# Second expert weights loaded as two whole rows a partition, in a transformer block with a mixture of experts

## The chip, the cores and the metric

The kernel runs on one core of a Trainium2 chip, as one launch. The metric is the time of the launch on the device in microseconds; lower is better. All data are float32 in the chip's memory (HBM); a core has an on-chip store of 128 partitions (SBUF), a smaller one for the results of products (PSUM), a matrix engine (TensorE, PE in the profile), three engines for elementwise work (VectorE as DVE, ScalarE as ACT, GpSimd as POOL), a synchronizing engine whose queue issues transfers (SyncE, SP), and 16 DMA engines that move the data.

## The reference, cut to what matters

Two transformer blocks on a sequence of 256 tokens of width 1024: a feed-forward layer, three kinds of attention and a second feed-forward layer; then a second block of long convolutions and a recurrence, and last a mixture of 16 experts, which is where the change lies. Each expert picks the 32 tokens that have the largest affinity to it:

```python
def expert_choice_moe(h, p):
    cap = EC_CAPACITY * T // N_EXPERTS                      # 2 * 256 // 16 = 32
    affinity = jax.nn.softmax((h @ p['router_w']).astype(jnp.float32), axis=-1)
    gates, idx = lax.top_k(jnp.swapaxes(affinity, 1, 2), cap)
    xe = jax.vmap(lambda hb, ib: hb[ib])(h, idx)
    hid = jax.nn.silu(jnp.einsum('becd,edf->becf', xe, p['exp_w1'])) * jnp.einsum('becd,edf->becf', xe, p['exp_w3'])
    ye = jnp.einsum('becf,efd->becd', hid, p['exp_w2']) * gates[..., None].astype(h.dtype)
    return jax.vmap(lambda ib, yb: jnp.zeros((T, D), yb.dtype).at[ib.reshape(-1)].add(yb.reshape(-1, D)))(idx, ye)
```

An expert's first and third weights (`exp_w1`, `exp_w3`) have 1024 rows of 2048 numbers, its second weights (`exp_w2`) 2048 rows of 1024 numbers. Each of the three is 8 MB, so the sixteen experts read 384 MB.

## The kernel before

Everything up to the mixture of experts takes a little over the first half of the time and is left as it is. The last function, `moe`, first finishes the token mixer's output, works out the affinities, and picks the tokens: `phr` holds for each expert a selection of 32 tokens, `ph` the same times the gates. `xeT` holds the chosen tokens of all experts, transposed.

Then a loop runs over the 16 experts. All weights of the experts come through one ring of 19 slots of 128 partitions x 2048 numbers (1 MB a slot). `wload` (line 1770) takes the next slot and issues one load of 1 MB on SP's queue; the order of the slots is fixed by `RINGS` and `RING_ORDER`, and a load waits until the products that read its slot's last content are done. There are 24 loads an expert: 8 of first weights, 8 of third weights, 8 of second weights.

First and third weights (lines 1780 to 1791): load k holds rows 128k to 128k+127, one row of 8 KB in each partition. The 32 chosen tokens of the expert are the stationary operand of products that fill 32 columns of the array; the four quarters g of the row go to four column groups, so `ps` holds quarter g in its partitions 32g to 32g+31.

Between them and the second weights (lines 1799 to 1814): the gated activation `th`, [32g + token, 512], four transposes of it (line 1805) that give `hid`, [128, q, 32g + token], and the transposed, gated selection `pgT`, which repeats each expert's 32 tokens four times over the partitions.

Second weights (lines 1815 to 1827): row f = 512g + 128q + p of the weights belongs to partition p of `hid`'s part (q, g). The output's 1024 columns are taken in two halves `nh` of 512. For each half and each q one load brings, for partition p, the four rows of g = 0 to 3, and of each row the half's 512 numbers: four pieces of 2 KB. Four products, one for each g, add into four column groups of one PSUM tile `pe2`. After the four loads of a half, ScalarE copies `pe2` to `ye` (line 1825), and two products over all 128 partitions (line 1827) sum the four groups, apply the gates, and scatter the tokens into the accumulators `acc[t][nh]` (t: the two blocks of 128 tokens), which add up over all experts.

After the last expert (lines 1828 to 1848): a row `m5p` is loaded behind the weights; for each of the four accumulators, in the order (nh, t) = (0,0), (0,1), (1,0), (1,1), ScalarE sums the squares and VectorE multiplies by `m5p`; then come two inverse norms, the residual, and four stores. The helper `then` (line 1635 in the profile) keeps the order of these operations on each engine.

The order of the loads is the order of the program's lines; the tile framework's scheduler orders the instructions of the engines.

Of the kernel before, what the change touches and what calls it, by code (L numbers as in the profile page):

```python
# [11 lines left out]
F32 = mybir.dt.float32  # L12
# [3 lines left out]
AF = mybir.ActivationFunctionType  # L16
# [6 lines left out]
NE = 16  # L23
# [142 lines left out]
def _body(nc, tc, ctx, A, out):  # L166
    V, S, G, PE = nc.vector, nc.scalar, nc.gpsimd, nc.tensor
# [9 lines left out]
    psT = ctx.enter_context(tc.tile_pool(name="psT", bufs=2, space=PSUM))  # L177
# [3 lines left out]
    def consts(name, shape, src=None, eng=None):  # L181
        t = keep.tile(list(shape), F32, name=name)
        (eng or S).dma_start(t, src if src is not None else A[name])
        return t
# [11 lines left out]
    ident = consts("ident", [128, 128])  # L196
# [1402 lines left out]
    def moe(xs, w1, po, m2p, xr, rw, m3c, a2c, last):  # L1599
        with ExitStack() as fx:  # L1600
# [13 lines left out]
            for k in range(KC):  # L1614
                PE.matmul(ps[:, :NE], m3c[:, k:k + 1].to_broadcast([128, 128]), rw[:, k, :], start=(k == 0),
                          stop=(k == KC - 1))
# [103 lines left out]
            def slot():  # L1720
                used[0] += 1
                return order[(used[0] - 1) % len(order)].tile([128, 2048], F32, name="ring")
# [12 lines left out]
            pt = psT.tile([128, 4, 128], F32, name="tr")  # L1735
# [7 lines left out]
            def select(half):  # L1743
                es = slice(half * HE, half * HE + HE)
                for t in range(2):
                    V.tensor_tensor(phr[:, t, es], pos[:, t, es].unsqueeze(2).to_broadcast([128, HE, CAP]),
                                    iota.unsqueeze(1).to_broadcast([128, HE, CAP]), op=ALU.is_equal)
                    G.tensor_tensor(ph[:, t, es], phr[:, t, es].bitcast(F32),
                                    aff[:, t, es].unsqueeze(2).to_broadcast([128, HE, CAP]), op=ALU.mult)

            def gather(half, k0, n):


                es = slice(half * HE, half * HE + HE)
                ps = psM.tile([128, 2, HE * CAP], F32, name="mm")
                for k in range(k0, k0 + n):
                    j = k - k0
                    for t in range(2):
                        for h_ in (h2h, h2l):
                            PE.matmul(ps[:, j, :], h_[t][:, k * 128:(k + 1) * 128], phr[:, t, es].rearrange("p a b -> p (a b)"),  # L1760
                                      start=(t == 0 and j == 0 and h_ is h2h), stop=(t == 1 and h_ is h2l),
                                      skip_group_check=True)
                    dst = xeT[:, k, half * HE * CAP:(half + 1) * HE * CAP]
                    if k % 2:
                        S.activation(dst, ps[:, j, :], AF.Identity, scale=a2c[:, k:k + 1], bias=m3c[:, k:k + 1])
                    else:
                        V.tensor_scalar(dst, ps[:, j, :], a2c[:, k:k + 1], m3c[:, k:k + 1], op0=ALU.mult, op1=ALU.add)


            def wload(src, shape):  # L1770
                r = slot()
                v = r.rearrange("p (a b) -> p a b", b=shape)
                with tc.issue_after(last):
                    nc.sync.dma_start(v, src)
                return v

            for e in range(NE):
                es = slice(e * CAP, (e + 1) * CAP)
                pss = []
                for nm in ("exp_w1_2", "exp_w3_2"):  # L1780
                    ps = psX.tile([128, 512], F32, name="px")
                    for k in range(KC):
                        if e == 0 and nm == "exp_w1_2" and k in GATHERS:
                            if k == 0:
                                select(0)
                            gather(0, k, GATHERS[k])
                        wt = wload(A[nm][e, k * 128:(k + 1) * 128, :].rearrange("p (a n) -> p a n", a=1), 2048)
                        for g in range(4):
                            PE.matmul(ps[32 * g:32 * g + 32, :], xeT[:, k, es], wt[:, 0, g * 512:(g + 1) * 512],  # L1789
                                      start=(k == 0), stop=(k == KC - 1), skip_group_check=True)  # L1790
                    pss.append(ps)
                    if e == 0 and nm == "exp_w1_2":
                        select(1)
                        for k in range(0, KC, 2):
                            gather(1, k, 2)
                        f2.close()
                        tmp = fx.enter_context(tc.tile_pool(name="moe_t", bufs=2))
                        acc = [[psM.tile([128, 512], F32, name="mm") for _ in range(2)] for _ in range(2)]
                th = tmp.tile([128, 512], F32, name="mth")
                S.activation(th, pss[0], AF.Tanh, scale=0.5)  # L1800
                V.scalar_tensor_tensor(th, th, 1.0, pss[0], op0=ALU.add, op1=ALU.mult)  # L1801
                V.scalar_tensor_tensor(th, th, 0.5, pss[1], op0=ALU.mult, op1=ALU.mult)  # L1802
                pt = psT.tile([128, 4, 128], F32, name="tr")
                for q in range(4):
                    PE.transpose(pt[:, q, :], th[:, q * 128:(q + 1) * 128], ident)
                hid = tmp.tile([128, 4, 128], F32, name="hid")
                V.tensor_copy(hid, pt)
                pt = psX.tile([128, 512], F32, name="px")
                for t in range(2):
                    rep = tmp.tile([128, 4, CAP], F32, name="rep")  # L1810
                    V.tensor_copy(rep, ph[:, t, e:e + 1, :].to_broadcast([128, 4, CAP]))
                    PE.transpose(pt[:, t * 128:(t + 1) * 128], rep.rearrange("p a b -> p (a b)"), ident)
                pgT = tmp.tile([128, T], F32, name="pgT")
                S.activation(pgT, pt[:, :T], AF.Copy)
                wv = A["exp_w2_2"][e].rearrange("(g q p) n -> q p g n", g=4, q=4)
                for nh in range(2):
                    ns = slice(nh * 512, nh * 512 + 512)
                    pe2 = psT.tile([128, 512], F32, name="tr")
                    for q in range(4):
                        w2t = wload(wv[q, :, :, ns], 512)  # L1820
                        for g in range(4):
                            PE.matmul(pe2[32 * g:32 * g + 32, :], hid[:, q, 32 * g:32 * g + 32], w2t[:, g, :],  # L1822
                                      start=(q == 0), stop=(q == 3), skip_group_check=True)
                    ye = tmp.tile([128, 512], F32, name="ye")
                    S.activation(ye, pe2, AF.Copy)  # L1825
                    for t in range(2):
                        PE.matmul(acc[t][nh], pgT[:, t * 128:(t + 1) * 128], ye, start=(e == 0), stop=(e == NE - 1))  # L1827
            m5p = slot()[:, 0:D]
            mod_row(m5p, 5, nc.sync)
            junk = slot()  # L1830
# [73 lines left out]

    ffn(xt, hT2, None, A["ffn2_w_gate"], A["ffn2_w_up"], A["ffn2_w_down"], {-1: filter_and_modulation, HOOK2: lambda: next(mods[1]), HOOK3: lambda: next(mods[1], None)}, norm_mod)
    moe(xt, w1, *mixer2(xt, hT3, *spec, spx, w1, rowp[0]))
```

## Time and profile before

| | |
|---|---|
| median of 3 runs | 2192.0 us (2189.52 to 2193.94) |
| profiled execution, its own time | 2195.16 us |
| its span, first to last instruction | 2193.4 us |
| mean granted TensorE clock | 0.86 |
| PE busy | 1784.5 us (81%) |
| DVE, ACT, POOL busy | 884.9, 589.9, 334.8 us |
| moved | 600.95 MB, mean 274 GB/s |
| loads of expert weights | 384 of 1024 KB |

The profile is of one execution. A time in it is in microseconds from the start of the span. An engine is busy while it executes; the profile names for an idle stretch what ended it (the releaser). A product in float32 leaves two records for each matmul instruction, so the four products on one load are eight records. The DMA share of a window is the sum of the times of all its packets over 16 engines, so it can be a little above 1. In an instruction's name, out<-in are the program's tile names; 128*32 is the part of the array that a product uses (rows * columns).

### The profile page before, as it was taken

What the parts mean: (1) busy time and instruction counts of PE and PEld (TensorE: products, weight loads), DVE (VectorE), ACT (ScalarE), POOL (GpSimd) and SP (SyncE); (2) the same over time, 40 slices, a digit from 0 to 9 for tenths busy, and PEclk for the clock granted to TensorE, in tenths of its full rate; (3) what the DMA queues carried; (4) which work ended last, traced back from release to release, by engine and by line L of the source; (5) the groups of instructions that cost most, each with busy time, mean ns of one, the idle gap of its engine ahead of it and who ended that gap; (6) DMA issues with size and microseconds to landing.
All of it is one profiled execution on the core that took longest, in us unless ns stands there. A gap on an engine that the chain in (4) does not pass through costs nothing.

```text
span 2193.4 us, 28407 instructions
## 1 busy us (share of the span) xinstructions
PE 1784.5 (81%) x11441; PEld 1067.1 (49%) x11442; DVE 884.9 (40%) x1611; ACT 589.9 (27%) x954; POOL 334.8 (15%) x332
## 2 busy tenths in 40 slices
PE   7999989999988999998898877766666676666765
PEld 5889867778768877886677411111111111111111
DVE  4567865965757765787655400000000000000001
ACT  3345443445436534363233200000000000000000
POOL 2111014110325640144233100000000000000000
PEclk9999989999989999999898887677778777777677
DMA  8655546444458846433347999999999999999997
GB/s 300 224 171 149 160 138 190 138 142 127 132 170 264 292 157 200 127 105 107 92 155 264 347 406 406 410 411 410 408 407 406 407 407 407 410 411 411 409 406 278
DMA packets 237046, 600.95 MB, mean 274 GB/s; under 512 B 35384, under 2 KB 91217, under 8 KB 204146
## 3 DMA queue, kind: packets, MB, share of 16 engines
q1 hardware_dynamic: 200464, 551.89, 68.6%
q0 software_dynamic: 10496, 36.08, 5.0%
q10 hardware_dynamic: 25954, 11.16, 1.9%
q8 instruction: 90, 1.47, 0.3%
q14 instruction: 42, 0.34, 0.0%
HBM read 593.25 MB, written 9.75 MB: 275 GB/s over the span
## 4 chain that ended last, share of the span: by engine, by line
DMA 43%; PE 39%; DVE 9%; ACT 3%; issue 3%; POOL 2%; SPq 0%; ACTq 0%; DVEq 0%; POOLq 0%
DMA ring<-exp_w 38%; PE mm L302 4%; PE mm L301 3%; PE mm L299 3%; PE mm L287 3%; PE mm L288 3%; PE mm L289 3%; DVE wl L246 2%; PE mm L346 2%; PE mm L349 2%; PE mm L345 2%; PE px L1789 2%; PE tr L1822 1%; DMA wraw<-w_in 1%; ACT wh L245 1%
## 5 line engine op out<-in xcount | busy, mean ns | idle before, releaser
L1789 PE MATMUL px<-ring,xeT 128*32 128x512 f32 x2048 | 365.5, 806 | 182.6 <-DMA ring<-exp_w 182.4
L246 DVE TENSOR_TENSOR wl<-wraw,wh 128x1024 fp32r<-128x1024 f32 (+2 forms) x243 | 317.8, 1309 | 169.0 <-ACT wh L245 163.4
L245 ACT ACTIVATE wh<-wraw 128x1024 fp32r<-128x1024 f32 (+2 forms) x243 | 254.9, 1050 | 378.9 <-PE mm L301 156.2
L302 PE MATMUL mm<-hh,wl 128*128 128x256 f32 x912 | 266.7, 294 | 16.1 <-DVE wl L246 15.1
L1789 PEld LDWEIGHTS px<-ring,xeT 128*32 128x32 f32 x2048 | 49.4, 122 | 469.2 <-DMA ring<-exp_w 427.8
L299 PE MATMUL mm<-hh,wh 128*128 128x256 f32 x912 | 265.0, 291 | 2.3 <-ACT hh L245 2.3
L301 PE MATMUL mm<-hl,wh 128*128 128x256 f32 x912 | 263.0, 289 | 1.9 <-DVE hl L246 1.8
L1801 DVE SCALAR_TENSOR_TENSOR mth<-mth,px 128x512 f32<-128x512 f32 x16 | 11.0, 688 | 576.4 <-ACT mth L1800 576.4
L1822 PE MATMUL tr<-ring,hid 128*32 128x512 f32 x1024 | 175.0, 791 | 76.7 <-DMA ring<-exp_w 64.0
L302 PEld LDWEIGHTS mm<-hh,wl 128*128 128x128 f32 x912 | 177.9, 196 | 31.2 <-DVE wl L246 20.0
L299 PEld LDWEIGHTS mm<-hh,wh 128*128 128x128 f32 x912 | 178.7, 196 | 11.6 <-issue 6.9
L301 PEld LDWEIGHTS mm<-hl,wh 128*128 128x128 f32 x912 | 178.6, 196 | 7.0 <-issue 4.1
L1825 ACT ACTIVATE ye<-tr 128x512 f32<-128x512 f32 x32 | 19.1, 598 | 573.2 <-PE tr L1822 573.2
L1635 POOL TENSOR_SCALAR rsz<-ss 128x1 f32<-128x1 f32 x2 | 0.6, 301 | 955.5 <-ACT ring L1635 955.5
L288 PE MATMUL mm<-wl,hh 128*128 128x512 f32 (+2 forms) x320 | 127.9, 400 | 5.3 <-DVE wl L271 3.3
L1822 PEld LDWEIGHTS tr<-ring,hid 128*32 128x32 f32 x1024 | 26.6, 126 | 206.4 <-DMA ring<-exp_w 153.5
L289 PE MATMUL mm<-wh,hl 128*128 128x512 f32 (+2 forms) x320 | 125.4, 392 | 0.0
L287 PE MATMUL mm<-wh,hh 128*128 128x512 f32 (+2 forms) x320 | 118.9, 404 | 5.2 <-DVE wi L525 3.3
L1802 DVE SCALAR_TENSOR_TENSOR mth<-mth,px 128x512 f32<-128x512 f32 x16 | 11.0, 688 | 257.4 <-PE px L1789 257.4
L1827 PE MATMUL mm<-ye,pgT 128*128 128x512 f32 x128 | 89.6, 838 | 24.0 <-ACT ye L1825 24.0
L1800 ACT ACTIVATE mth<-px 128x512 f32<-128x512 f32 x16 | 9.6, 597 | 283.1 <-PE px L1789 283.1
L1827 PEld LDWEIGHTS mm<-ye,pgT 128*128 128x128 f32 x128 | 29.1, 252 | 88.1 <-ACT ye L1825 63.6
(757 smaller groups left out, 2735.8 us busy)
## 6 DMA issues: line engine op xcount, KB each, us to landing
ring<-exp_w SPq DMA_DIRECT2D x384, 1024.0 KB
wraw<-w_in SPq DMA_DIRECT2D x107, 512.0 KB
mraw<-mod_w POOLq DMA_DIRECT2D x48, 512.0 KB, 5.1
wraw<-ffn_w_gate SPq DMA_DIRECT2D x44, 512.0 KB
wraw<-ffn_w_up SPq DMA_DIRECT2D x44, 512.0 KB
wraw<-ffn_w_down SPq DMA_DIRECT2D x44, 512.0 KB
wraw<-w_out SPq DMA_DIRECT2D x11, 512.0 KB
skew<-bd POOLq DMA_DIRECT2D x1, 3840.0 KB, 27.3
```

Source lines behind the costliest of these rows:

```text
L245: S.activation(dst_h, src, AF.Copy)
L246: (eng or V).tensor_tensor(dst_l, src, dst_h.bitcast(F32), op=ALU.subtract)
L287: PE.matmul(ps[t], hh[:, k, sl], wh, start=(k == 0), stop=False)
L288: PE.matmul(ps[t], hh[:, k, sl], wl, start=False, stop=False)
L289: PE.matmul(ps[t], hl[:, k, sl], wh, start=False, stop=(k == kc - 1))
L299: PE.matmul(o(c), wh[:, cs], hh[:, k, :], start=(k == 0 and bank0(c)), stop=False, skip_group_check=True)
L301: PE.matmul(o(c), wh[:, cs], hl[:, k, :], start=False, stop=False, skip_group_check=True)
L302: PE.matmul(o(c), wl[:, cs], hh[:, k, :], start=False, stop=(k == KC - 1), skip_group_check=True)
L345: PE.matmul(acc[t][nh], fh[:, sl], wh[:, ns], start=(k == 0), stop=False)
L1789: PE.matmul(ps[32 * g:32 * g + 32, :], xeT[:, k, es], wt[:, 0, g * 512:(g + 1) * 512], start=(k == 0), stop=(k == KC - 1), skip_group_chec ...
L1822: PE.matmul(pe2[32 * g:32 * g + 32, :], hid[:, q, 32 * g:32 * g + 32], w2t[:, g, :], start=(q == 0), stop=(q == 3), skip_group_check=True)
L1827: PE.matmul(acc[t][nh], pgT[:, t * 128:(t + 1) * 128], ye, start=(e == 0), stop=(e == NE - 1))
```

## The change

The second weights' 2048 rows are assigned to the partitions in another order, so that a load brings whole rows. Row f = 512g + 4p + 2h + j now belongs to partition p. A load (g, h) brings for partition p the two rows j = 0 and 1, which lie next to each other in memory, so 8 KB; from one partition to the next the step is 16 KB. To match, the transposes of `th` take every fourth element (`th[:, q::4]`) in place of 128 neighbours, so that part q = 2h + j of `hid` holds those rows. A load's four products are now for the two rows j and the two output halves nh; they go to the column groups 2nh + j, in the order 0, 2, 1, 3, and all 32 products of an expert add into one tile `pe2`. There is one copy `ye` per expert in place of two, and the four products with `pgT` use 64 partitions each, nh = 0 the lower and nh = 1 the upper ones, alternating, with the sum over j in the contraction.

```diff
--- before.py
+++ after.py
@@ -1802,7 +1802,7 @@
                 V.scalar_tensor_tensor(th, th, 0.5, pss[1], op0=ALU.mult, op1=ALU.mult)
                 pt = psT.tile([128, 4, 128], F32, name="tr")
                 for q in range(4):
-                    PE.transpose(pt[:, q, :], th[:, q * 128:(q + 1) * 128], ident)
+                    PE.transpose(pt[:, q, :], th[:, q::4], ident)
                 hid = tmp.tile([128, 4, 128], F32, name="hid")
                 V.tensor_copy(hid, pt)
                 pt = psX.tile([128, 512], F32, name="px")
@@ -1812,19 +1812,25 @@
                     PE.transpose(pt[:, t * 128:(t + 1) * 128], rep.rearrange("p a b -> p (a b)"), ident)
                 pgT = tmp.tile([128, T], F32, name="pgT")
                 S.activation(pgT, pt[:, :T], AF.Copy)
-                wv = A["exp_w2_2"][e].rearrange("(g q p) n -> q p g n", g=4, q=4)
-                for nh in range(2):
-                    ns = slice(nh * 512, nh * 512 + 512)
-                    pe2 = psT.tile([128, 512], F32, name="tr")
-                    for q in range(4):
-                        w2t = wload(wv[q, :, :, ns], 512)
-                        for g in range(4):
-                            PE.matmul(pe2[32 * g:32 * g + 32, :], hid[:, q, 32 * g:32 * g + 32], w2t[:, g, :],
-                                      start=(q == 0), stop=(q == 3), skip_group_check=True)
-                    ye = tmp.tile([128, 512], F32, name="ye")
-                    S.activation(ye, pe2, AF.Copy)
-                    for t in range(2):
-                        PE.matmul(acc[t][nh], pgT[:, t * 128:(t + 1) * 128], ye, start=(e == 0), stop=(e == NE - 1))
+
+
+                wv = A["exp_w2_2"][e].rearrange("(g p h j) n -> g h p (j n)", g=4, h=2, j=2)
+                pe2 = psT.tile([128, 512], F32, name="tr")
+                for g in range(4):
+                    for h in range(2):
+                        w2t = wload(wv[g, h], 512)
+                        for j in range(2):
+                            for nh in range(2):
+                                c = nh * 2 + j
+                                PE.matmul(pe2[32 * c:32 * c + 32, :], hid[:, 2 * h + j, 32 * g:32 * g + 32],
+                                          w2t[:, j * 2 + nh, :], start=(g == 0 and h == 0), stop=(g == 3 and h == 1),
+                                          skip_group_check=True)
+                ye = tmp.tile([128, 512], F32, name="ye")
+                S.activation(ye, pe2, AF.Copy)
+                for t in range(2):
+                    for nh in range(2):
+                        r = slice(nh * 64, nh * 64 + 64)
+                        PE.matmul(acc[t][nh], pgT[r, t * 128:(t + 1) * 128], ye[r, :], start=(e == 0), stop=(e == NE - 1))
             m5p = slot()[:, 0:D]
             mod_row(m5p, 5, nc.sync)
             junk = slot()
```

## Rows read from the trace of the kernel before

**Rows 1.** The page's slices: the span in 40 equal parts of 54.8 us.
```profile
DMA  8655546444458846433347999999999999999997
...
GB/s 300 224 171 149 160 138 190 138 142 127 132 170 264 292 157 200 127 105 107 92 155 264 347 406 406 410 411 410 408 407 406 407 407 407 410 411 411 409 406 278
```

**Rows 2.** The chain that ended last, from 1150 us on, by line.
```profile
by line: DMA ring<-exp_w 80.8%; PE px L1789 3.2%; PE tr L1822 2.9%; PE mm L1760 1.0%; issue 1.0%; SPq L1774 0.8%; PE tr L1805 0.8%; PE mm L1551 0.8%; PE mm L1553 0.8%; PE mm L1552 0.8%; PE mm L1827 0.7%; DVE mth L1802 0.5%; DVE hid L1807 0.
```

**Rows 3.** Windows: us, busy per engine, PE clock, DMA share, GB/s; three stretches.
```profile
1150.00:1170.00 20.00, 15.67 (x61) 12.45 (x60) 15.74 (x29) 12.95 (x22) 10.41 (x7) 0.83 0.69 234
...
2031.00:2053.00 22.00, 15.03 (x76) 3.21 (x80) 1.38 (x2) 0.60 (x1) 0.00 (x0) 0.73 1.05 394
...
2053.00:2093.00 40.00, 28.57 (x138) 4.50 (x136) 1.05 (x3) 1.58 (x3) 0.00 (x0) 0.69 1.01 416
```

**Rows 4.** Timeline of PE over one expert: start, us, line, operation, [idle before <-releaser].
```profile
2031.20 1.94 PE L1789 MATMUL px<-ring,xeT 128*32 128x512 f32 x8 [0.60 <-DMA ring<-exp_w]
...
2033.94 1.12 PE L1805 MATMUL tr<-ident,mth 128*128 128x128 f32 x4 [0.81 <-DVE mth L1802]
...
2050.12 1.77 PE L1822 MATMUL tr<-ring,hid 128*32 128x512 f32 x8 [1.60 <-DMA ring<-exp_w]
...
2052.81 1.94 PE L1822 MATMUL tr<-ring,hid 128*32 128x512 f32 x8 [0.92 <-DMA ring<-exp_w]
...
2092.77 1.07 PE L1789 MATMUL px<-ring,xeT 128*32 128x512 f32 x8 [0.97 <-DMA ring<-exp_w]
```

**Rows 5.** The page's DMA queues: packets, MB, share of 16 engines; and packet sizes.
```profile
q1 hardware_dynamic: 200464, 551.89, 68.6%
...
q10 hardware_dynamic: 25954, 11.16, 1.9%
...
DMA packets 237046, 600.95 MB, mean 274 GB/s; under 512 B 35384, under 2 KB 91217, under 8 KB 204146
```

**Rows 6.** Windows at the first expert's loads, columns as in Rows 3.
```profile
1230.00:1240.00 10.00, 10.00 (x76) 4.63 (x73) 1.09 (x2) 1.61 (x3) 0.00 (x0) 0.94 0.81 288
...
1240.00:1250.00 10.00, 10.00 (x82) 4.59 (x82) 1.56 (x3) 1.19 (x3) 0.00 (x0) 1.00 1.05 377
```

**Rows 7.** Waits of SP's queue from 1150 us on: us in total, times, longest.
```profile
SPq L1774 <- DMA ring<-exp_w: 407.4, 207, 3.2
```

**Rows 8.** Timeline of all engines at the end, last expert.
```profile
2155.28 1.93 PE L1789 MATMUL px<-ring,xeT 128*32 128x512 f32 x8 [0.61 <-DMA ring<-exp_w]
...
2165.34 2.53 SPq L885 DMA_DIRECT2D ring<-mrows  x1
...
2169.04 0.60 ACT L1635 ACTIVATE ring<-mm 128x512 f32<-128x512 f32 x1 [1.22 <-PE mm L1827]
...
2169.90 0.60 ACT L1635 ACTIVATE ring<-mm 128x512 f32<-128x512 f32 x1 [0.17 <-PE mm L1827]
...
2176.77 1.93 PE L1822 MATMUL tr<-ring,hid 128*32 128x512 f32 x8 [1.59 <-DMA ring<-exp_w]
...
2178.41 1.29 DVE L1635 TENSOR_TENSOR ring<-mm,ring 128x512 f32<-128x512 f32 x2 [18.54 <-DMA ring<-mrows]
...
2178.83 0.60 ACT L1825 ACTIVATE ye<-tr 128x512 f32<-128x512 f32 x1 [8.24 <-PE tr L1822]
...
2179.48 3.78 PE L1827 MATMUL mm<-ye,pgT 128*128 128x512 f32 x4 [0.78 <-ACT ye L1825]
...
2181.59 0.60 ACT L1635 ACTIVATE ring<-mm 128x512 f32<-128x512 f32 x1 [2.17 <-PE mm L1827]
...
2183.36 0.60 ACT L1635 ACTIVATE ring<-mm 128x512 f32<-128x512 f32 x1 [1.08 <-PE mm L1827]
...
2184.08 0.69 DVE L1635 TENSOR_TENSOR ring<-mm,ring 128x512 f32<-128x512 f32 x1 [1.07 <-ACT ring L1635]
```

**Rows 9.** Timeline of PE: products of half the array's rows, and whole-array transposes.
```profile
378.55 0.72 PE L592 MATMUL px<-kiT,qiT 64*128 64x128 f32 x8
...
414.31 0.66 PE L254 MATMUL mm<-ident,qn 128*128 128x128 f32 x4
```

## Prediction, made before the change was run

> **What bounds the kernel now.** I read the slices first: from slice 22 (1206 us) the DMA digit is 9 in every slice but the last, and from 1261 us the rate stays at 406 to 411 GB/s until the last [rows 1]; this is the stage of the sixteen experts. The chain that ended last, cut to the part behind 1150 us, says the same from the other side: 80.8% of it is the landing of the experts' weights (ring<-exp_w), and no product line has more than 3.2% [rows 2]. PE is busy in that stage and is still not what it waits for: in the timeline of one expert each group of products on a fresh tile begins at a landing, after an idle gap of 0.6 to 1.6 us [rows 4]. So a microsecond saved in the landings of this stage is a microsecond of the end, as long as the DMA engines always have the next load queued. They have: the DMA share is 1.01 and 1.05 in the windows of one expert [rows 3], and SP, which issues all these loads, waited 407.4 us in that stretch for earlier landings [rows 7], so it runs ahead of the transfers.
>
> The next view is the one that decides. The window that holds mostly second weights (2031 to 2053) moves 394 GB/s at a share of 1.05, the window of first and third weights (2053 to 2093) 416 GB/s at 1.01 [rows 3]: the second weights move fewer bytes and keep the engines busier. In single loads: the last third-weight load of one expert is taken up at 2031.20 and the last of its eight second-weight loads at 2052.81, so 21.61 us for 8, 2.70 each; the sixteen loads after it end at 2092.77, 39.96 us, 2.4975 each [rows 4]. All are 1 MB. The last expert repeats it: 2155.28 to 2176.77 is 21.49 us [rows 8].
>
> **Why a second-weight load is slower.** A first- or third-weight load reads 8 KB in one piece per partition, a second-weight load four pieces of 2 KB. The page counts 32,900 packets of 8 KB or more (237,046 less 204,146) [rows 5], and 256 loads of 128 such rows make 32,768, so one row is one packet. Two queue lines give the price of a packet: q1 took 68.6% of 16 engines' 2193.4 us for 200,464 packets, 120 ns each at 2,753 bytes on average, and q10 1.9% for 25,954, 25.7 ns each at 430 bytes [rows 5]. A line through the two has a fixed part of about 8.2 ns a packet (7.4 to 9.1 by the rounding of 1.9%) and 0.0406 ns a byte. One of 16 engines carries 64 KB of a load: 32 packets of 2 KB or 8 of 8 KB, so 24 packets fewer are 0.18 to 0.22 us. The landings differ by 0.204 us. Two views that share no number agree, so I take the difference to be the count of packets.
>
> **The change part by part.**
> *Shape of the loads.* Count and bytes stay: 8 loads of 1 MB an expert. Each now reads 8 KB in one piece per partition, the pieces 16 KB apart. I take the pace of the other 8 KB loads, 2.4975 us [rows 4]. Fifteen experts have all eight of their second-weight loads in the stretch that DMA bounds: 15 x (21.61 - 8 x 2.4975) = 15 x 1.63 = 24.4 us. For the first expert the ring's 19 slots are filled ahead: its 16 first and third loads and 3 second loads wait for PE and gain nothing. The other five land while the share goes from 0.81 to 1.05 [rows 6], so DMA bounds most of them: 5 x 0.204 = 1.0 us (bounds 0 and 1.0). Sum: 25.4 us.
>
> *Products on the second weights.* 32 an expert as before, each 32 columns of the array, in four different column groups one after the other. A load's four products (8 records) take 1.1 to 1.9 us and PE then idles 0.6 to 1.6 us until the next landing [rows 4]; I cost them at nothing, for 1.9 is still less than the new distance of 2.4975. A slot of the ring is given back after its own four products, as now.
>
> *Transposes of th with a step of four elements.* No row shows that stride. The four take 1.12 us [rows 4]; they stand in front of eight loads, of which one has landed by then (they end 3.9 us after 2031.20, and a load takes 2.70), and PE takes up the rest as they land. Even at three times their time, 2.2 us more, PE has caught up before the eighth landing. Nothing; upper bound 2.2 us once, at the last expert, if it had not.
>
> *One copy of the product (ye) instead of two, and four products over half the array's rows instead of four over all rows.* ACT's copy now waits for all eight loads, not for four; behind it on ACT stands only the next expert's tanh, which needs eight further loads, so nobody is held up. Inside the stage this is hidden under the loads. Products that use opposite halves of the rows run in pairs: eight records of such products take 0.72 us against 0.66 for four whole-array ones of the same 128 columns [rows 9]. So the four cost what two do now.
>
> *The end.* This cover is gone after the last landing. Now the left half (nh = 0) is finished long before: its second square starts at 2169.90, and after the last landing at 2176.77 only the right half is left: products 1.93, copy at 2178.83, two products of 3.78 us together, squares at 2181.59 and 2183.36, multiply at 2184.08 [rows 8]. After the change all four sums become ready there. With pairs, the first two at the time of 2181.59 and the last two at that of 2183.36. ACT works in the order left t0, left t1, right t0, right t1, and the second of these waits for the second pair, so three squares stand behind 2183.36 in place of one: two more at the spacing of 0.86 us (from 2169.04 to 2169.90) make 1.7 us, which I take. If the pairs did not overlap, the products would take 3.5 us more instead (two more of 1.77, the distance of 2181.59 and 2183.36) [rows 8]. Bounds 1.7 and 3.5. The row m5p for the multiply is issued after the last weight load and was there at 2178.41 [rows 8], 3 us before it is needed.
>
> *The sum.* 25.4 - 1.7 = 23.7 us. The profiled execution took 2195.16 us (span 2193.4), 3.2 above the median of the runs; from its own time the sum leads to 2171.5, and from the median, which is what I forecast, to 2192.0 - 23.7 = 2168.3. The loads' pace alone, with the fixed part at 7.4 or 9.1 ns, gives 22 to 27 us, so 2166 to 2173 with the end at either bound.
>
> **The rivals.** The pace after the change, P, decides all; the time is 2193.7 - 125 x (2.70 - P), where 125 is the number of second loads in the bound stretch and 2193.7 the median with the longer end.
> 1. *Only a part is packets.* Part of the 0.204 us comes from where the pieces lie, and pieces 16 KB apart keep some of it. For it: no load here has 8 KB pieces with gaps between. Against: the packet price from the queue lines fills the whole difference. At half, P = 2.60: 2181. The Trainium skill, "DMA: Bandwidth & Descriptors", section "Why small descriptors are slow", gives about 3 cycles a packet on beats of 32 bytes; at the page's 850 MHz that is, as an estimate from it, 3.5 ns, 24 packets 0.085 us, a gain of 10.6 less 1.7 and a time of 2183. The queue lines here give 8.2 ns, more than twice as much.
> 2. *The pace does not change.* The tile that is written is still seen as four blocks of 512, and a load that were cut along it would go in 2 KB packets as now; or 2 KB is long enough and the difference has another cause. Time 2193.7. Against: [rows 5] and the landings. The Trainium skill's same page, "Specifications", puts line rate at 512 bytes and above; by that rule the change leaves the pace and costs the end. The trace does not agree: the 2 KB loads land 8% slower [rows 4].
> 3. *Slower: the gaps cost more than the packets.* Every load skips each second 8 KB of a 2 MB region, and memory may serve that worse than rows end to end. The point from which it decides is P = 2.69 (the end eats 1.7 us, 0.014 a load); beyond 2.72 it is slower by over 0.2%. For a price: the window with most engine time per GB/s here is 0.69 at 234 against 1.01 at 416 [rows 3], 21% more; P = 3.03 and a time of 2235. Against: the present loads skip half of each 4 KB row too, and their pace is explained without it.
>
> **How the numbers follow.** Forecast, packets explain all: 0.73, its own range 2165 to 2173. Rival 1: 0.09. Rival 2: 0.07. Rival 3: 0.06. A larger gain (pairs hide more of the end, or the fixed part is larger): 0.05, 2160 to 2165. The range 2163 to 2182 leaves out rivals 2 and 3 and the outer edges. About 0.2%, 4.4 us, is what a measurement of this kernel can tell. Faster by more: forecast, rival 1 but its edge, and the larger gain, 0.85; within: rival 2 and that edge, 0.08; slower: 0.07.
>
> **What would show it.** Right: packets under 8 KB fall by some 65,500 (128 loads x 128 x 4), those of 8 KB rise by 16,400; the distance between landings is 2.50 us for all three weights; windows of second weights show a share of 1.01 and about 416 GB/s; an expert takes 60.0 us instead of 61.6. At the end the distance from last landing to end of span, 16.6 us now, is 18 to 20. Wrong: the packet counts stay (rival 2); the counts change and the distance is 2.55 to 2.69 (rival 1) or above 2.69 (rival 3); or PE begins groups without waiting for a landing, which would mean that the transposes or half-row products took longer than the loads leave room for.

## The result and the profile after

The changed kernel takes 2169.5 us, median of 4 runs (2165.86 to 2171.2), against 2192.2 us for the kernel before, median of 4: a ratio of 0.9895, with a 95% interval of 0.9878 to 0.9913. It is faster by 22.7 us; the forecast was 23.7 us and 2168.3 us.

The profiled execution took 2165.86 us with a span of 2164.1 us. The page after: slices of 54.1 us, packet sizes, and the queue of the weights.

```profile
DMA  9665555454448855534445899999999999999996
GB/s 303 217 184 142 159 147 177 138 146 127 136 146 269 274 194 174 156 94 124 121 137 218 338 420 420 420 420 420 420 420 420 419 420 419 420 420 420 420 419 270
DMA packets 187894, 600.95 MB, mean 278 GB/s; under 512 B 35384, under 2 KB 91217, under 8 KB 138610
...
q1 hardware_dynamic: 151312, 551.89, 67.5%
```

The experts' slices move 419 to 420 GB/s where they moved 406 to 411 [rows 1]. Packets under 8 KB fell by 65,536 and those of 8 KB and more rose by 16,384 [rows 5]: four pieces became one, in every second-weight load. The chain that ended last, behind 1150 us, says that the bound is still the same one, and more so (80.8% before [rows 2]):

```profile
by line: DMA ring<-exp_w 88.7%; PE px L1789 1.4%; PE mm L1760 0.9%; PE mm L1551 0.8%; PE mm L1553 0.8%; PE mm L1552 0.8%; issue 0.6%; PE mm L1833 0.4%; PE px L1669 0.4%; PE mm L254 0.3%; DVE x L1588 0.2%; DVE wl L246 0.2%; DVE ring L1635 0.
```

Two windows of one expert after, columns as in [rows 3]: the eight second-weight loads, then the sixteen first and third ones.

```profile
2005.00:2025.00 20.00, 11.81 (x72) 1.96 (x69) 1.38 (x2) 0.00 (x0) 0.00 (x0) 0.83 1.01 420
2025.00:2065.00 40.00, 26.80 (x142) 3.93 (x138) 1.13 (x3) 1.58 (x3) 0.00 (x0) 0.74 1.01 420
```

Before, the two differed, 394 GB/s at a share of 1.05 against 416 at 1.01; now they are alike. In single loads, the timeline of PE over the same expert (columns as in [rows 4]):

```profile
2004.85 1.07 PE L1789 MATMUL px<-ring,xeT 128*32 128x512 f32 x8 [0.97 <-DMA ring<-exp_w]
2006.73 0.75 PE L1805 MATMUL tr<-ident,mth 128*128 128x128 f32 x4 [0.81 <-DVE mth L1802]
...
2022.30 1.80 PE L1825 MATMUL tr<-ring,hid 128*32 128x512 f32 x8 [0.56 <-DMA ring<-exp_w]
2024.79 1.06 PE L1825 MATMUL tr<-ring,hid 128*32 128x512 f32 x8 [0.69 <-DMA ring<-exp_w]
...
2064.69 1.89 PE L1789 MATMUL px<-ring,xeT 128*32 128x512 f32 x8 [1.43 <-DMA ring<-exp_w]
```

From the last third-weight load to the last second-weight load 19.94 us, then 39.90 us: 2.49 us a load in both. Over the fifteen experts whose second weights DMA bounds, the median of that stage fell from 21.60 to 19.95 us. PE still waits for a landing in front of the groups shown.

SP's queue behind 1150 us (us in total, times, longest) waits for earlier landings longer than in [rows 7]. Behind the third expert, whenever it issues a load, at least eight loads (this one counted) are issued and not yet taken up by PE, so the DMA engines always have loads queued:

```profile
SPq L1774 <- DMA ring<-exp_w: 743.1, 352, 3.1
```

The end, all engines, answering to [rows 8]:

```profile
2146.04 1.93 PE L1825 MATMUL tr<-ring,hid 128*32 128x512 f32 x8 [0.56 <-DMA ring<-exp_w]
2148.10 0.60 ACT L1829 ACTIVATE ye<-tr 128x512 f32<-128x512 f32 x1 [37.52 <-PE tr L1825]
...
2148.75 3.79 PE L1833 MATMUL mm<-ye,pgT 64*128 64x512 f32 x8 [0.78 <-ACT ye L1829]
...
2150.86 0.60 ACT L1635 ACTIVATE ring<-mm 128x512 f32<-128x512 f32 x1 [2.16 <-PE mm L1833]
...
2152.57 0.60 ACT L1635 ACTIVATE ring<-mm 128x512 f32<-128x512 f32 x1 [1.02 <-PE mm L1833]
...
2153.15 0.59 ACT L1635 ACTIVATE ring<-mm 128x512 f32<-128x512 f32 x1
2153.29 1.89 DVE L1635 TENSOR_TENSOR ring<-mm,ring 128x512 f32<-128x512 f32 x3 [1.02 <-ACT ring L1635]
2153.63 0.20 ACT L1635 ACTIVATION_READ_ACCUMULATOR ring<-mm 128x1 f32 x1
2153.72 0.60 ACT L1635 ACTIVATE ring<-mm 128x512 f32<-128x512 f32 x1
```

From the last landing to the end of the span it is 18.0 us (2146.04 to 2164.09), 16.6 before.

The two profiled executions differ by 29.3 us of span. Of it 4.5 lie ahead of the first expert product (1228.67 to 1224.14 us), in code that did not change; 26.2 lie between that product and the last landing (948.1 to 921.9); the end gives 1.4 back.

### The profile page after: what moved, and what is told of

Read it like the earlier page. It is cut to its first block, busy times and chain, and to the rows that moved or that the text cites. A ratio compares the mean times of both kernels' runs of the same rounds, so it can differ in the third digit from the quotient of the medians.

```text
span 2164.1 us, 28403 instructions
## 1 busy us (share of the span) xinstructions
PE 1736.5 (80%) x11441; PEld 1048.8 (48%) x11442; DVE 885.5 (41%) x1611; ACT 579.1 (27%) x938; POOL 335.5 (16%) x332
## 4 chain that ended last, share of the span: by engine, by line
DMA 45%; PE 37%; DVE 9%; ACT 3%; issue 3%; POOL 2%; ACTq 0%; DVEq 0%; SPq 0%; POOLq 0%
DMA ring<-exp_w 42%; PE mm L302 4%; PE mm L301 4%; PE mm L299 4%; PE mm L287 3%; PE mm L288 3%; PE mm L289 3%; DVE wl L246 3%; PE mm L346 2%; PE mm L349 2%; PE mm L345 2%; DMA wraw<-w_in 1%; ACT wh L245 1%; PE mm L254 1%; PE px L839 1%
## 5 line engine op out<-in xcount | busy, mean ns | idle before, releaser
L1789 PE MATMUL px<-ring,xeT 128*32 128x512 f32 x2048 | 356.7, 789 | 185.2 <-DMA ring<-exp_w 185.2
L1825 PE MATMUL tr<-ring,hid 128*32 128x512 f32 x1024 | 182.1, 813 | 101.8 <-DMA ring<-exp_w 89.1
L1829 ACT ACTIVATE ye<-tr 128x512 f32<-128x512 f32 x16 | 9.6, 597 | 559.6 <-PE tr L1825 559.6
L288 PEld LDWEIGHTS mm<-wl,hh 128*128 128x128 f32 x320 | 61.4, 192 | 18.9 <-DVE wl L246 3.2
L287 PEld LDWEIGHTS mm<-wh,hh 128*128 128x128 f32 x320 | 59.4, 193 | 20.5 <-issue 7.7
```

Source lines behind the costliest of these rows:

```text
L287: PE.matmul(ps[t], hh[:, k, sl], wh, start=(k == 0), stop=False)
L288: PE.matmul(ps[t], hh[:, k, sl], wl, start=False, stop=False)
L1825: PE.matmul(pe2[32 * c:32 * c + 32, :], hid[:, 2 * h + j, 32 * g:32 * g + 32], w2t[:, j * 2 + nh, :], start=(g == 0 and h == 0), stop=(g = ...
```

## The experiments

Two causes could make a second-weight load of the old shape slower than the others: theory 1, each piece has a fixed price; theory 2, it is where the pieces lie in memory. The change altered both. Each experiment starts from the changed kernel; the pace is the median over fifteen experts of the second-weight stage, divided by its 8 loads.

**The new rows in 2 KB pieces** (e1_same_place_2k). Every load still reads the same 8 KB a partition, but its target in the ring has a gap of 16 numbers behind each 512, which cuts the row into four pieces. A slot grows to 2112 numbers and the ring has 18 slots in place of 19.

```diff
-                return order[(used[0] - 1) % len(order)].tile([128, 2048], F32, name="ring")
+                return order[(used[0] - 1) % len(order)].tile([128, 2112], F32, name="ring")
...
-                v = r.rearrange("p (a b) -> p a b", b=shape)
+                v = r.rearrange("p (a b) -> p a b", b=2112 * shape // 2048)[:, :, :shape]
...
-                wv = A["exp_w2_2"][e].rearrange("(g p h j) n -> g h p (j n)", g=4, h=2, j=2)
+                wv = A["exp_w2_2"][e].rearrange("(g p h j) (i b) -> g h p (j i) b", g=4, h=2, j=2, i=2)
```

> The changed kernel with one thing undone: each second-weight load still reads the same 8 KB of two whole rows for every partition, in the same order, but writes it to four blocks of 512 numbers with a gap of 16 numbers between them, so that it cannot go in pieces longer than 2 KB. To make room for the gaps the ring has 18 slots in place of 19; first and third loads stay single rows of 8 KB and serve as the control inside the run. Theory 1 (the old pace came from the number of packets, 8.2 ns each): landings of second weights 2.49 + 24 x 0.0082 = 2.69 us apart, share of DMA 1.05 in their windows, first and third weights still 2.49; time 2169.5 + 125 x 0.20 = about 2194. Theory 2 (the old pace came from the place: half rows, four regions 2 MB apart): 2.49 us apart as in the changed kernel, time about 2170.

Measured: 2198.8 us, ratio to the kernel before 1.0024 (1.0005 to 1.0043). The packet counts are those of before to the last one, and so is the pace, 2.700 us. Its page, PE at four of its second-weight loads, 2.67 to 2.70 apart, and two windows (columns as in [rows 3]) of second and of first and third weights:

```profile
DMA packets 237046, 600.95 MB, mean 273 GB/s; under 512 B 35384, under 2 KB 91217, under 8 KB 204146
```

```profile
1992.04 1.68 PE L1825 MATMUL tr<-ring,hid 128*32 128x512 f32 x8 [1.65 <-DMA ring<-exp_w]
1994.74 1.93 PE L1825 MATMUL tr<-ring,hid 128*32 128x512 f32 x8 [1.02 <-DMA ring<-exp_w]
1997.41 1.94 PE L1825 MATMUL tr<-ring,hid 128*32 128x512 f32 x8 [0.73 <-DMA ring<-exp_w]
2000.10 1.94 PE L1825 MATMUL tr<-ring,hid 128*32 128x512 f32 x8 [0.75 <-DMA ring<-exp_w]
```

```profile
1984.00:2002.00 18.00, 13.11 (x64) 1.44 (x56) 0.00 (x0) 0.00 (x0) 0.00 (x0) 0.59 1.05 399
2006.00:2040.00 34.00, 23.76 (x124) 3.24 (x122) 1.13 (x3) 0.98 (x2) 0.00 (x0) 0.70 1.01 415
```

The new places with the old pieces lose the whole gain. Theory 2 falls. The first and third weights, which this run leaves in pieces of 8 KB, keep their pace of 2.497 us, so the smaller ring does not slow those. The gap in the target is not the cause either: the kernel before has the same pace without one.

The time is 4.8 us above the expected 2194 and 6.6 above the kernel before. In the profiles 2.7 us of that lie between the first product and the second expert's last third-weight load (62.9 against 60.2) and 1.4 in the longer end. Where the rest lies, and whether the ring's missing slot costs the 2.7, is not shown.

**The new rows in 1 KB pieces** (e3_same_place_1k). As e1, with `i=4` and a gap behind each 256 numbers; a product then reads its 512 columns as 2 x 256.

> As the run with pieces of 2 KB in the changed kernel's places, but eight blocks of 256 numbers, so pieces of 1 KB: the suspected cost more than doubled. Products read two blocks of 256 in place of one of 512. Theory 1: 64 packets per engine in place of 8, 2.49 + 56 x 0.0082 = 2.95 us apart; time about 2169.5 + 125 x 0.46 = 2227. Theory 2: 2.49 apart, time about 2170. A rule by which pieces of 512 bytes and more all go at one rate also says 2.49.

Measured: 2230.2 us, ratio 1.0164 (1.0137 to 1.0191); pace 2.916 us, as PE shows over four loads (11.66 us):

```profile
DMA packets 302582, 600.95 MB, mean 270 GB/s; under 512 B 35384, under 2 KB 222289, under 8 KB 269682
```

```profile
2002.80 1.06 PE L1825 MATMUL tr<-ring,hid 128*32 128x512 f32 x8 [1.22 <-DMA ring<-exp_w]
...
2014.46 1.93 PE L1825 MATMUL tr<-ring,hid 128*32 128x512 f32 x8 [0.98 <-DMA ring<-exp_w]
```

**Two rows of 4 KB, 128 rows apart** (e2_rows_4k). The transposes of `th` read neighbours again, as before the change.

```diff
-                    PE.transpose(pt[:, q, :], th[:, q::4], ident)
+                    PE.transpose(pt[:, q, :], th[:, q * 128:(q + 1) * 128], ident)
...
-                wv = A["exp_w2_2"][e].rearrange("(g p h j) n -> g h p (j n)", g=4, h=2, j=2)
+                wv = A["exp_w2_2"][e].rearrange("(g h j p) n -> g h p j n", g=4, h=2, j=2)
```

> Second weights as whole rows of 4 KB: a load brings rows 128 apart for j = 0 and 1, two pieces of 4 KB per partition, and together one region of 1 MB without gaps; the transposes take 128 neighbours as in the kernel before. Theory 1 (packets, 8.2 ns each): 16 packets per engine in place of 8, so 2.49 + 8 x 0.0082 = 2.56 us apart; time about 2169.5 + 125 x 0.066 = 2178. Theory 2 (place): whole rows without gaps, so 2.49 apart or a little less, time 2170 or below.

Measured: 2175.0 us, ratio 0.9903 (0.9874 to 0.9933); 204,278 packets; pace 2.556 us. PE from the last third-weight load of an expert to its last second-weight load, 20.44 us:

```profile
2014.48 1.93 PE L1789 MATMUL px<-ring,xeT 128*32 128x512 f32 x8 [0.57 <-DMA ring<-exp_w]
...
2034.92 1.94 PE L1825 MATMUL tr<-ring,hid 128*32 128x512 f32 x8 [0.59 <-DMA ring<-exp_w]
```

**8 KB pieces without gaps** (e4_no_gaps_8k). A load takes 256 neighbouring rows, 1 MB end to end; the transposes step by two.

```diff
-                    PE.transpose(pt[:, q, :], th[:, q::4], ident)
+                    PE.transpose(pt[:, q, :], th[:, (q // 2) * 256 + q % 2:(q // 2) * 256 + 256:2], ident)
...
-                wv = A["exp_w2_2"][e].rearrange("(g p h j) n -> g h p (j n)", g=4, h=2, j=2)
+                wv = A["exp_w2_2"][e].rearrange("(g h p j) n -> g h p (j n)", g=4, h=2, j=2)
```

> The changed kernel without the gaps in memory: partition p of a load takes rows 2p and 2p+1 of 256 neighbouring rows, so a load is one region of 1 MB end to end, still one piece of 8 KB per partition; the transposes take every second element in place of every fourth. Theory 1 (packets): 2.49 us apart as now, time 2165 to 2172, no difference from the changed kernel. Rival (gaps of 8 KB cost something that the packets' saving hides): landings below 2.48, time below 2165.

Measured: 2168.8 us, ratio 0.9889 (0.9865 to 0.9914); pace 2.494 us, the same as with the gaps. PE over the same stage, 19.95 us:

```profile
2008.81 1.94 PE L1789 MATMUL px<-ring,xeT 128*32 128x512 f32 x8 [0.56 <-DMA ring<-exp_w]
...
2028.76 1.93 PE L1825 MATMUL tr<-ring,hid 128*32 128x512 f32 x8 [1.43 <-DMA ring<-exp_w]
```

Pieces 16 KB apart cost nothing that these landings show.

**16 KB pieces** (e5_rows_16k). The other direction: four whole rows a partition, 2 MB a load, in a ring of 9 slots of 2 MB; two first- or third-weight loads share a slot. Of its edit only the line of the addresses is shown; the ring, `wload` and the loop of the products change to match.

```diff
-                wv = A["exp_w2_2"][e].rearrange("(g p h j) n -> g h p (j n)", g=4, h=2, j=2)
+                wv = A["exp_w2_2"][e].rearrange("(g p i) n -> g p (i n)", g=4, i=4)
```

> One step further in the direction of the change: the ring has 9 slots of 2 MB, a second-weight load brings four whole rows, one piece of 16 KB per partition and 2 MB end to end; first and third weights go two loads to a slot, still in pieces of 8 KB. Theory 1 (a fixed price per packet, 7.5 to 8.6 ns by the runs with 4, 2 and 1 KB): 4 packets fewer per engine and MB, so the eight MB of second weights take 19.95 - 8 x 4 x 0.0078 = 19.7 us in place of 19.95, 4.0 us less over the kernel; at the end eight products in place of four stand behind the last landing, 1.9 us more; time about 2167. Rival (a packet is never longer than 8 KB, or the price ends there): 19.95 us and a time of about 2171.

Measured: 2173.1 us, ratio 0.9901 (0.988 to 0.9923). The packets fell to 178,676, and PE takes up loads of 2 MB 4.91 and 4.92 us apart, against 4.99 for two loads after the change:

```profile
2021.81 3.64 PE L1834 MATMUL tr<-ring,hid 128*32 128x512 f32 x16 [1.17 <-DMA ring<-exp_w]
2026.72 1.92 PE L1834 MATMUL tr<-ring,hid 128*32 128x512 f32 x16 [1.27 <-DMA ring<-exp_w]
2031.64 2.96 PE L1834 MATMUL tr<-ring,hid 128*32 128x512 f32 x16 [3.00 <-DMA ring<-exp_w]
```

Most second-weight stages took 19.64 us in place of 19.95, but two of the fifteen 21.15. From the second expert's last third-weight load to the last landing it is 857.5 us against 862.5. The first two experts took 5.9 us more (65.3 against 59.4 from the first product to that load). Why they did is not shown. That eats the gain: the stage from the first product to the last landing is 922.7 against 921.9. So the expected pace came (19.7 us) and the expected time of 2167 did not; the 3.5 us by which the median lies above the changed kernel's are inside the spread of e5's runs (2164.4 to 2178.3).

**The written order of the half-row products** (e6_same_halves): both products of the left half first, then both of the right, so that neighbours use the same array rows.

```diff
-                for t in range(2):
-                    for nh in range(2):
+                for nh in range(2):
+                    for t in range(2):
```

> The changed kernel with the four products on the half rows of the array in another order: both of nh = 0, then both of nh = 1, so that two neighbours mostly use the same half. If opposite halves run in pairs only when they stand next to each other, the eight records that take 1.99 us (fast clock) and 3.79 us (slow clock) now take about 3.0 and 5.6 us (only the middle two overlap); if the engine pairs them whatever the order, they stay. Either way hidden under the loads but for the last expert: the end behind the last landing is then 18.1 + 1.0 to 1.8 us, and the time 2169.5 to 2171.5, no difference that can be measured.

Measured: 2168.8 us, ratio 0.9883 (0.9867 to 0.9899). PE and ACT at its end:

```profile
2152.39 1.99 PE L1833 MATMUL mm<-ye,pgT 64*128 64x512 f32 x8 [0.79 <-ACT ye L1829]
...
2153.55 0.60 ACT L1635 ACTIVATE ring<-mm 128x512 f32<-128x512 f32 x1 [1.21 <-PE mm L1833]
...
2154.40 0.60 ACT L1635 ACTIVATE ring<-mm 128x512 f32<-128x512 f32 x1 [0.17 <-PE mm L1833]
```

The products still run in pairs: the eight records take 1.99 us with the clock granted in full. The second square waits for the product that is written second, and comes 0.85 us after the first square, so that product ran with the second pair: a product of the other half had gone ahead of it. Whether the lowering of the program or the engine does that, these rows do not say. The run shows that this written order is no cost, not what unpaired products would cost.

**The squares in the order of the products** (e7_squares_in_order): `t` outer and `nh` inner in the loop at line 1840, so that a square never waits for the second pair while one of the first pair is ready behind it.

> The changed kernel with the squares and multiplies behind the last expert in the order in which its products end: both halves of t = 0, then both of t = 1. The second square no longer waits for the second pair, so one square and one multiply leave the end: 18.05 us from the last landing to the end of the span become about 17.4. Time 2169, no difference from the changed kernel that can be measured. If the end were bound by the multiplies on VectorE and not by the squares, it would stay at 18.05.

Measured: 2167.8 us, ratio 0.9882 (0.9868 to 0.9897). Its end:

```profile
2153.86 3.79 PE L1833 MATMUL mm<-ye,pgT 64*128 64x512 f32 x8 [0.78 <-ACT ye L1829]
...
2155.97 0.60 ACT L1635 ACTIVATE ring<-mm 128x512 f32<-128x512 f32 x1 [2.16 <-PE mm L1833]
...
2156.68 0.60 ACT L1635 ACTIVATE ring<-mm 128x512 f32<-128x512 f32 x1
...
2157.67 0.60 ACT L1635 ACTIVATE ring<-mm 128x512 f32<-128x512 f32 x1 [0.30 <-PE mm L1833]
...
2158.39 0.60 ACT L1635 ACTIVATE ring<-mm 128x512 f32<-128x512 f32 x1
```

The last square starts 4.53 us after the products start, against 4.97 after the change (2148.75 to 2153.72), and from last landing to end of span it is 17.3 us against 18.0, with products of 3.79 us in both. The time is 1.7 us below the changed kernel's, which is inside the spread of either's runs (5.3 and 3.9 us).

## Why the prediction was right, point by point

**DMA bounds the stage, so a landing saved is time saved.** It held. The changed landings account for 23.9 us of the profiled execution (fifteen second-weight stages, 324.2 to 300.3 us), where the forecast had 24.4; the medians of the runs differ by 22.7.

**The price of a piece.** This was the step that decided, and it held. With the bytes of a load and its place in memory kept (e1, e3), the pace goes with the number of pieces; e2, with no gap on either side, lies on the same line. One DMA engine carries 8 pieces of 8 KB of a load, or 16, 32 or 64 smaller ones:

| piece | pieces per engine | pace, us a MB | over 8 KB, ns a piece more |
|---|---|---|---|
| 16 KB (e5) | 4 | 2.455 | 9.7 saved for each fewer |
| 8 KB (changed kernel, e4) | 8 | 2.494 | |
| 4 KB (e2) | 16 | 2.556 | 7.8 |
| 2 KB (e1) | 32 | 2.700 | 8.6 |
| 1 KB (e3) | 64 | 2.916 | 7.5 |

The last column is the difference in pace divided by that in pieces: (2.700 - 2.494) / 24 is 8.6 ns. The forecast read 8.2 ns (7.4 to 9.1) off two queue lines of the kernel before [rows 5]. That it met the landings so closely is in part luck. Its line gives the difference between the loads but not their level: 32 packets of 2 KB come to 2.92 us and 8 of 8 KB to 2.73, where the loads land every 2.70 and 2.49. And a third queue of that page does not lie on it: q0 took 167 ns a packet at 3,437 bytes on average, where the line has 148.

```profile
q0 software_dynamic: 10496, 36.08, 5.0%
```

The packets' own durations in the trace, medians behind 1300 us, agree in kind: 313 ns for 8 KB, 164 for 4 KB, 87 for 2 KB, 48 for 1 KB, so about 10 ns that do not shrink with the bytes (48 less 1,024 times the 0.037 ns a byte between 48 and 313). The landings lose a little less than these durations say, for the packets of an engine overlap: 64 of 48 ns are 3.07 us, and the load lands every 2.92.

**A rival that was not named: the issuing.** SP, too, spent longer on a load of four pieces. Its issues of all 384 loads, before and after (count: min, median and max in ns):

```profile
L1774 SPq DMA_DIRECT2D ring<-exp_w x384: 327/378/8084, 1156.1 to 2162.7; - x192
```

```profile
L1774 SPq DMA_DIRECT2D ring<-exp_w x384: 327/328/644, 1150.9 to 2125.6; - x192
```

It did not set the pace. Behind the third expert never fewer than six loads of the kernel before were issued and not yet taken up (counted as above), and in the windows of second weights the packets fill the engines' time, at a share of 1.05 both before [rows 3] and in e1.

**Rival 1, only a part is packets.** It needed a pace of 2.60; measured 2.494. The Trainium skill, "DMA: Bandwidth & Descriptors", section "Why small descriptors are slow", has the mechanism, a fixed overhead for each, and the runs agree; its figure of about 3 cycles, 3.5 ns as an estimate, is less than half of the 7.5 to 9.7 ns here, and the measurement decides.

**Rival 2, the pace does not change.** The packet counts and the landings changed. The same page's section "Specifications", by which 512 bytes are enough for line rate, does not hold for these loads: pieces of 1 KB land 17% slower than pieces of 8 KB, pieces of 4 KB still 2.5%.

**Rival 3, the gaps cost more.** e4 has no gaps and the same pace.

**First expert, 1.0 us.** Not shown. Its second-weight stage lasts 10.21 us with pieces of 1, 2 and 8 KB alike (e3, e1, the changed kernel) and 12.17 before, with pieces of 2 KB as in e1, so its landings do not set it, and a slower pace appears only in the loads behind it. From the first product to the second expert's last third-weight load it is 60.2 us before and 59.4 after, but 57.7 in e4 and 60.0 in e6, whose loads have the same pace. That the landings' sum came out near its 25.4 us is in part luck: the 26.2 us between first product and last landing are 23.9 in the fifteen second-weight stages, 0.8 here, and 1.4 in the fourteen stages of first and third weights (563.7 to 562.3), for which the forecast had nothing. Their cause stays open.

**Products and transposes at nothing.** They held. The four transposes take 0.75 us in the expert shown after, with a granted clock of 1.00, and 1.13 in the last one, with 0.50. With neighbouring elements they take 0.66 and 1.11 us at the same two clocks, here in two experts of e2:

```profile
1349.76 0.66 PE L1805 MATMUL tr<-ident,mth 128*128 128x128 f32 x4 [0.82 <-DVE mth L1802]
1410.49 1.11 PE L1805 MATMUL tr<-ident,mth 128*128 128x128 f32 x4 [0.81 <-DVE mth L1802]
```

So the step of four elements costs 0.09 us an expert at the full clock and 0.02 at half of it, and the loads hide it. In the expert shown PE waits for the landing in front of each of the last seven second-weight loads.

**The end.** The mechanism held and the size was slightly off: 1.4 us longer, forecast 1.7. The term was two squares at a spacing of 0.86 us; that spacing held a wait of 0.17 us for a product [rows 8]. Without a wait the squares start 0.57 us apart (2153.15 and 2153.72): the next one starts before the readout of the sum, 2153.63 to 2153.83, is over. The first two squares are a pair's length apart, 1.71 us, as forecast. So the last square starts 1.1 us later behind the last landing than before (7.7 against 6.6), and the other 0.3 us lie behind it, where the forecast had nothing. The second inverse norm now falls due while GpSimd (POOL) is busy with the first: it starts 0.6 us after the last readout ends (2154.41 to 2154.98), and before it was 0.1. e7 takes 0.8 us of this back.

## What to carry to other kernels

Where transfers bound a stage, count the contiguous pieces of a load as well as its bytes, contiguous on both sides (in e1 a gap in the target alone cuts the row into four): here each piece cost about 8 ns of a DMA engine, so a contraction whose rows may be assigned freely should give each partition neighbouring rows. The price can be read before the change, from two kinds of load with equal bytes, and more roughly from two queues of different piece size on the page; it pays to check that both agree. What the new assignment moves behind the last landing is paid in full, and its order is worth a look of its own.

## What the runs showed that was not expected

The end's length depends on the clock that the last products get. With a granted clock of 0.50 (1.2 GHz) the four half-row products took 3.79 us and the end 18.0 to 18.1 us (changed kernel, e1, e2, e3). With 1.00 (2.4 GHz) they took 1.99 us and the end 15.9 and 16.1 us (e4, e6). Just before, the granted clock was 0.69 and 0.72 (2130 to 2148 us of the changed kernel, 2134 to 2152 us of e6), so these means do not tell which of the two it will be. Which of the two an execution meets moves the time by about 2 us, more than any edit of the end here. In the kernel before it was 0.50 as well (2178 to 2183.3 us), so the 1.4 us above compare like with like.

The window of the end in the changed kernel, and in e6 (columns as in [rows 3]):

```profile
2148.70:2152.60 3.90, 3.79 (x8) 1.18 (x8) 0.69 (x1) 0.72 (x3) 0.00 (x0) 0.50 0.00 0
```

```profile
2152.30:2154.40 2.10, 1.99 (x8) 0.71 (x8) 0.14 (x1) 0.72 (x3) 0.00 (x0) 1.00 0.00 0
```

The first expert product starts anywhere from 1224.14 to 1235.69 us in the profiles, behind code that none of these kernels changes. That is half of the effect under study, and a reason to compare stages and not single spans.
